# Keeping plain float32 blocks of the first token half in a two-layer trunk kernel

## The chip, the cores and the metric

The kernel runs on one core of one Trainium2 chip. The metric is the device time of one execution in microseconds (us). The engines of the core work side by side and wait for each other through semaphores: TensorE (PE in the profile, with its weight loads as PEld) multiplies matrices, VectorE (DVE) and ScalarE (ACT) work element by element, GpSimd (POOL) does the same more slowly, and SyncE (SP) issues most of the DMAs. TensorE writes its products into PSUM banks; all else lies in SBUF tiles.

## The reference

The program is a trunk of two layers on 1024 tokens of width 1024. Layer 0 mixes tokens with a gated delta net, layer 1 with retention; behind each mixer stands a convolutional feed-forward block. Cut to what matters here:

```python
e = jax.nn.silu(c @ cond_w + cond_b)
for i in range(DEPTH):
    mod = (e @ ada_w[i] + ada_b[i])[:, None, :]
    sh1, sc1, g1, sh2, sc2, g2 = jnp.split(mod, 6, axis=-1)
    y = mixers[i % N_MIXERS](x * (1.0 + sc1) + sh1)
    x = layer_norm(DN_ALPHA * x + (1.0 + g1) * y, ln_g[i, 0], ln_b[i, 0])
    y = conv_ffn(x * (1.0 + sc2) + sh2, ffn_up[i], ffn_conv_w[i], ffn_conv_b[i], ffn_down[i])
    x = layer_norm(DN_ALPHA * x + (1.0 + g2) * y, ln_g[i, 1], ln_b[i, 1])
```

The change lies where `x * (1 + sc) + sh` is made ready for the large products behind it: for `ffn_up` of both layers and for the retention's `w_in`.

## The kernel before

**Products in three parts.** Every large float32 product is made of products of a faster type (`float32r`): each operand is split into a high half, a copy in that type by ScalarE (line 89), and a low half, the rest, by a subtraction on VectorE (line 90). Three products, low by high, high by low and high by high, then give one (`mm3`, lines 108 to 112).

**The stages.** Three times an input of 8 feature blocks by 1024 tokens meets a weight: stage A (feed-forward of layer 0), B (retention) and C (feed-forward of layer 1). The blocks are feature-major, 128 features by 512 tokens. With f the feature block (0 to 7) and k from 0 to 3, block 11 is f = k of the first token half, 21 is f = 4 + k of the first half, 12 and 22 are the same of the second half.

**The build.** The blocks of the first half (11 and 21) are made by `build_one` (line 279) while the projection before is still running on the second half: four transposes on TensorE into an mm bank (line 282), a scale and shift by ScalarE into a tile `tmp` of tag "t2" (line 284), and the split. In A that projection is `proj_ln`, in B and C it is `proj_gen`, which calls the build as hooks in its sixth product.

**The seven-product scheme.** `strassen` (line 1290) first computes two pairs of weight units in the plain way, by `side`: over the first half, and, when the second half's blocks are there, over the second half (line 1309). All other items run through `wino` (line 1357 and on), which needs seven products instead of eight and, for that, the sums T1 = 12 - 11, T3 = 22 - 12, T2 = T3 + 11 and T4 = 21 - T2. `build_T` makes the blocks 12 and 22 (transposes at line 439, scale and shift at line 441, splits); its inner function `rest`, called between the two side products of the second half, makes the T blocks. There the plain values of 12 and 22 are still at hand (`raw`), but those of 11 and 21 exist only as two halves. `whole` puts such a block together again: two products of a unit matrix with the high and with the low half, added in an mm bank (line 457), 8 blocks or 16 products per stage.

For each k, `rest` then runs on VectorE and ScalarE: a sum (line 464), the split of T3, a sum with block 11 from the bank (466), the split of T2, a sum (468), the split of T1, a sum with block 21 from the bank (470), the split of T4. Each split is a copy on ScalarE followed by the subtraction on VectorE.

**Buffers.** Tiles are taken from rings by tag: "t2" has 3 buffers, "qkv" 20, of 128x512 float32 each, mm has 2 PSUM banks. "qkv" holds the T3 and T4 blocks (16 buffers in the end), four of the raw blocks, and in the projection of B and C the loads and the halves of the last steps. In A and C, the T1, T2 and 12 blocks share the 8 buffers of "hTb".

**Order.** Instructions stand on each engine in an order that the framework's scheduler makes from the order of the program, the dependences, the free buffers and its own estimate of durations; each engine works its list in order. Only parts of the mixers and of the retention's output projection (`run`, `pq`) have an order written out by hand. `anchor` marks an instruction behind which others on the same engine are to stand.

Of the kernel before, what the change touches and what calls it, by code (L numbers as in the profile page):

```python
# [10 lines left out]
F32R = mybir.dt.float32r  # L11
AF = mybir.ActivationFunctionType
ALU = mybir.AluOpType
AX = mybir.AxisListType

P = 128
D = 1024
S = 1024
KT = D // P
HALF = 512  # L20
# [8 lines left out]
BAL = {"r11": 0, "r12": 0, "r22": 0, "rS1": 0, "rS2": 0, "rS3": 0, "rS4": 0, "rw21": 0, "rwT1": 0, "rwT2": 0, "rwT3": 0, "rwT4": 0, "rn": 0, "rh": 1, "011": 0, "012": 0, "022": 0, "0S1": 0, "0S2": 0, "0S3": 0, "0S4": 0, "0w21": 0, "0wT1": 0, "0wT2": 0, "0wT3": 0, "0wT4": 0, "0n": 1, "0h": 0, "f11": 0, "f12": 0, "f22": 0, "fS1": 0, "fS2": 0, "fS3": 0, "fS4": 0, "fw21": 0, "fwT1": 0, "fwT2": 0, "fwT3": 0, "fwT4": 0, "fn": 1, "fh": 0, "gw": 99, "gh": 0, "gn": 3, "b1": 0, "b2": 0, "b3": 0, "b4": 0, "bT": 0, "ba": 0, "rw11": 0, "rw22": 0, "0w11": 0, "0w22": 0, "fw11": 0, "fw22": 0}  # L29
# [4 lines left out]
def trunk_kernel(ctx: ExitStack, tc, A):  # L34
    nc = tc.nc
    pe, act, dve, pool, sp = nc.tensor, nc.scalar, nc.vector, nc.gpsimd, nc.sync
# [9 lines left out]
    def tl(tag, shape, dt=F32, name=None):  # L46
        return sb.tile(shape, dt, tag=tag, name=name or tag, bufs=BUFS[tag])

    def two(tag, dt=F32, name=None):
        if tag in ("qkv", "auh"):  # L50
            return tl(tag, [P, HALF], dt, name), tl(tag, [P, HALF], dt, name)
        t = tl(tag, [P, 2, HALF], dt, name)
        return t[:, 0], t[:, 1]
# [7 lines left out]
    def mm_tile():  # L61
        return ps.tile([P, HALF], F32, tag="mm", name="mm", bufs=2)
# [25 lines left out]
    def split(dst_h, dst_l, src, eng=dve):  # L88
        anchor["sp"] = act.activation(dst_h, src, AF.Copy)  # L89
        eng.tensor_tensor(dst_l, src, dst_h, ALU.subtract)  # L90

    anchor = {}
# [74 lines left out]
    def col_sum(a, n, tile):  # L167
        pt = tile()
        for j in range(n):
            pe.matmul(pt[:, j:j + 1], a[:, j * P:(j + 1) * P], ones[:, 0:1], start=True, stop=True)  # L170
        return pt
# [22 lines left out]
    ident, m_incl, m_low = [cst[:, i * P:(i + 1) * P] for i in range(3)]  # L194
# [5 lines left out]
    pt = col_sum(a0, NV, mm_tile)  # L200
# [75 lines left out]
        dve.tensor_add(shift, shift, sh)  # L276
        return scale, shift

    def build_one(tag, xts, scale, shift, f, eng=dve):
        pt = mm_tile()  # L280
        for t in range(4):
            pe.transpose(pt[:, t * P:(t + 1) * P], xts[t][:, f * P:(f + 1) * P], ident)
        tmp = tl("t2", [P, HALF])
        act.activation(tmp, pt, AF.Identity, bias=shift[:, f:f + 1], scale=scale[:, f:f + 1])
        ht = two(tag, F32R, "hT")
        split(ht[0], ht[1], tmp, eng)
        return ht

    def build_hT(tag, xts, scale, shift, fr=range(KT)):
        return [build_one(tag, xts, scale, shift, f) for f in fr]  # L290
# [93 lines left out]
    def ln_store(half, t, xts, dst, key):  # L384
        r0 = half * HALF + t * P
        anchor[key] = act.dma_start(dst[r0:r0 + P, :], xts[t])
# [31 lines left out]

    def ln_hooks(half, xts, tag, vecs2, out, dst, key, npool=0):
        def build(f):  # L420
            out.append(build_one(tag, xts, *vecs2(), f, pool if f < npool else dve))
        return ([lambda f=f: build(f) for f in range(KT)]
                + [lambda t=t: ln_store(half, t, xts, dst, key) for t in range(4)])

    def build_T(B, xts, scale, shift, tags):
        tags = dict(zip(("T1", "T2", "T3", "T4", "22"), tags))
        tags["12"] = tags["T1"]
        for nm in tags:
            B[nm] = [None] * 4

        def put(nm, k, src, eng=dve):
            t = two(tags[nm], F32R, nm)
            split(t[0], t[1], src, eng)
            B[nm][k] = t

        def load(f, tag):
            pt = mm_tile()
            for t in range(4):
                pe.transpose(pt[:, t * P:(t + 1) * P], xts[t][:, f * P:(f + 1) * P], ident)
            tmp = tl(tag, [P, HALF], name="bt")  # L440
            act.activation(tmp, pt, AF.Identity, bias=shift[:, f:f + 1], scale=scale[:, f:f + 1])
            return tmp

        raw = []
        for k, tg in enumerate((("qkv", "qkv"), ("qkv", "qkv"), ("t2", "t2"), ("t2", "ada"))):
            b12, b22 = load(k, tg[0]), load(4 + k, tg[1])
            put("12", k, b12, pool if BAL["b3"] & 1 << k else dve)
            put("22", k, b22, pool if BAL["b2"] & 1 << k else dve)
            raw.append((b12, b22))

        one = tl("S", [P, P], F32R, name="one")
        act.activation(one, ident, AF.Copy)

        def whole(b, k):
            pt = mm_tile()
            for i, x in enumerate(B[b][k]):
                pe.matmul(pt, one, x, start=(i == 0), stop=(i == 1))
            return pt

        def rest():  # L460
            for k in range(4):
                t1, b22 = raw[k]
                x11 = whole("11", k)
                dve.tensor_sub(b22, b22, t1)
                put("T3", k, b22, pool if BAL["b3"] & 1 << k else dve)
                dve.tensor_add(b22, b22, x11)
                put("T2", k, b22, pool if BAL["bT"] & 1 << k else dve)
                dve.tensor_sub(t1, t1, x11)
                put("T1", k, t1, pool if BAL["b1"] & 1 << k else dve)
                dve.tensor_sub(b22, whole("21", k), b22)  # L470
                put("T4", k, b22)

        return rest

# [815 lines left out]
    def strassen(hT0, xts, scale, shift, items, tags=("hTb", "hTb", "qkv", "qkv", "aux"), direct=False, late=()):  # L1290
# [23 lines left out]
        for n in (1, 0):  # L1314
# [11 lines left out]
            for t, x in zip(ahead[n], X):  # L1326
                act.activation(t, x, AF.Copy)
        rest = build_T(B, xts, scale, shift, tags)

        def block(src):  # L1330
# [463 lines left out]
    for nh in range(2):  # L1794
        pt = mm_tile()
# [16 lines left out]
    h0, xts = layer_tail(0, raws, A["gdn_wout"], xin, xs[0], xs[1], next0, False)  # L1812
# [46 lines left out]
    def gate_item(u):  # L1859
        def start():  # L1860
            def sink(q, a, b):
                c = c_of(q, a, b) if b is not None else tl("cv", [P, 516], name="sg")[:, 0:HALF]
                act.activation(c, a if b is None else c, AF.Silu)
                act.dma_start(gd[u + q // 2][:, hs(q % 2)], c)
            return sink
        return A["ret_wg"][u], A["ret_wg"][u + 1], start, None
# [5 lines left out]
    B = strassen(h0, xts, sc_r, sh_r, [gate_item(0), gate_item(2)] + mixed, ("hTa", "aux", "qkv", "qkv", "hTa"), True)  # L1872
    hT = [h0, []]
    xlo = []
    for t in range(4):
        x = tl("cv", [P, 516], name="xlo")[:, 0:HALF]
# [302 lines left out]
```

## Time and profile before

| | |
|---|---|
| time, median of 3 runs | 2877.69 us (2877.47 to 2882.09) |
| profiled execution, first to last instruction | 2868.4 us, 38930 instructions |
| granted TensorE clock, mean | 0.995 |
| unit-matrix products in stage A | 737.4 to 762.7 us |
| in stage B | 1406.0 to 1431.6 us |
| in stage C | 2232.3 to 2259.4 us |

The page gives the profiled execution by its span, from the first to the last instruction; its own time is not listed apart. Times in rows are us from the start of the span unless a row gives mean nanoseconds. `mm<-hT,one` reads: writes tile mm, reads tiles hT and one. A group's row ends with the engine's idle time in front of the group and what ended most of it. In an order of time, the square bracket holds the idle time just before that instruction and its releaser.

### The profile page before, as it was taken

The page shows a single profiled execution, that of the slowest core. Times are in us where ns is not written, and L with a number is a line of the kernel's source. Part 1 is how long each engine was busy: PE and PEld are TensorE (multiplying, and loading weights), DVE is VectorE, ACT ScalarE, POOL GpSimd, SP SyncE. Part 2 cuts the span into 40 slices and gives each one's busy share as a digit, 9 for nine tenths or more (in the row PEclk, how much of TensorE's full clock was granted, in tenths as well). Part 3 has the DMA queues.
Part 4 walks back from the last instruction along what each step waited for, and adds up shares of the span by engine and source line. Part 5 has one row for each costly group of instructions (what it writes and reads, how often), then busy time and mean ns, then how long its engine had stood idle before and what let it go on. Part 6 is the DMA issues. An engine that isn't in the chain of part 4 may idle for free.

```text
span 2868.4 us, 38930 instructions
## 1 busy us (share of the span) xinstructions
PE 2780.8 (97%) x13594; PEld 2273.7 (79%) x13594; DVE 2177.9 (76%) x3874; ACT 1298.0 (45%) x2387; POOL 499.8 (17%) x513
## 2 busy tenths in 40 slices
PE   8999999999999999999999999999999999999997
PEld 6788878887787878887788887777777788888886
DVE  6787778676788888868687656666689887777779
ACT  4664465344645444545433342222344644445543
POOL 0311321000023322000000002333201033332201
PEclk9999999999999999999999999999999999999999
DMA  7223242174255554855343364665754253444753
GB/s 279 89 96 122 92 139 90 64 255 148 96 186 176 189 181 164 299 161 182 129 147 125 118 202 153 200 209 159 256 200 150 74 195 132 144 140 165 285 184 116
DMA packets 252884, 465.30 MB, mean 162 GB/s; under 512 B 24144, under 2 KB 77776, under 8 KB 252688
## 3 DMA queue, kind: packets, MB, share of 16 engines
q1 hardware_dynamic: 218560, 408.02, 43.0%
q10 hardware_dynamic: 31488, 46.15, 4.4%
q0 software_dynamic: 2640, 8.65, 0.8%
q8 instruction: 107, 1.75, 0.2%
q14 instruction: 89, 0.73, 0.1%
HBM read 346.86 MB, written 115.87 MB: 161 GB/s over the span
## 4 chain that ended last, share of the span: by engine, by line
PE 61%; DVE 20%; DMA 9%; ACT 5%; issue 4%; POOL 1%; SPq 0%; ACTq 0%; DVEq 0%; POOLq 0%
PE acc L716 11%; PE acc L1296 6%; PE acc L110 5%; PE acc L111 4%; PE acc L112 4%; PE sc L716 4%; PE sc L1296 3%; PE acc L1596 3%; PE mm L716 2%; DVE o L1742 2%; DVE wb L90 2%; PE sc L110 2%; PE sc L112 2%; PE sc L111 2%; DMA mvw<-in_ada_w 1%
## 5 line engine op out<-in xcount | busy, mean ns | idle before, releaser
L716 PE MATMUL acc<-hT,wh 128*128 128x512 f32 x960 | 299.4, 393 | 0.0
L1596 PE MATMUL acc<-bb,ab 128*128 128x512 f32 x984 | 229.7, 392 | 7.0 <-DVE ab L90 4.7
L89 ACT ACTIVATE ab<-ar 128x512 fp32r<-128x512 f32 x210 | 131.2, 630 | 221.3 <-PE mm L303 52.1
L1596 PEld LDWEIGHTS acc<-bb,ab 128*128 128x128 f32 x984 | 183.0, 188 | 49.0 <-DVE ab L90 4.2
L716 PEld LDWEIGHTS acc<-hT,wh 128*128 128x128 f32 x960 | 182.0, 190 | 35.5
L90 DVE TENSOR_TENSOR ab<-ar,ab 128x512 fp32r<-128x512 f32 x210 | 147.4, 707 | 76.5 <-ACT ab L89 76.3
L1296 PE MATMUL acc<-T,wb 128*128 128x512 f32 x840 | 202.0, 389 | 0.4 <-DVE wb L90 0.4
L89 ACT ACTIVATE wb<-mm 128x512 fp32r<-128x512 f32 x216 | 124.4, 597 | 166.0 <-DVE mm L1350 154.5
L716 PE MATMUL acc<-hT,wl 128*128 128x512 f32 x480 | 196.2, 409 | 2.2 <-ACT sq L509 2.2
L1296 PEld LDWEIGHTS acc<-T,wb 128*128 128x128 f32 x840 | 157.5, 188 | 33.8 <-ACT o L1743 1.2
L90 DVE TENSOR_TENSOR wl<-wr,wh 128x1024 fp32r<-128x1024 f32 x98 | 122.2, 1247 | 74.6 <-ACT wh L89 74.0
L1773 POOL TENSOR_TENSOR o<-o 128x512 f32<-128x512 f32 x80 | 126.2, 1586 | 266.4 <-ACT pc L1366 173.1
L90 DVE TENSOR_TENSOR wb<-wr,wb 128x512 fp32r<-128x512 f32 x162 | 115.3, 713 | 67.6 <-ACT wb L89 67.5
L89 ACT ACTIVATE wh<-wr 128x1024 fp32r<-128x1024 f32 x98 | 103.8, 1060 | 137.1 <-PE acc L716 56.4
L1742 DVE SCALAR_TENSOR_TENSOR o<-g,vc,o 128x512 f32<-128x512 f32 (+2 forms) x176 | 148.8, 855 | 8.4 <-ACT o L1737 7.1
L90 DVE TENSOR_TENSOR wb<-mm,wb 128x512 fp32r<-128x512 f32 x216 | 144.6, 682 | 7.8 <-ACT wb L89 7.8
L89 ACT ACTIVATE wb<-wr 128x512 fp32r<-128x512 f32 x162 | 101.1, 626 | 95.4 <-PE acc L1296 27.5
L1350 DVE TENSOR_TENSOR mm<-wr 128x512 f32<-128x512 f32 x108 | 83.6, 774 | 70.3 <-DMA wr<-in_ffn_up 57.7
L716 PE MATMUL acc<-wh,hT 128*128 128x512 f32 x384 | 134.3, 412 | 2.1 <-DVE vv L90 2.1
L1366 ACT ACTIVATE pc<-acc 128x512 f32<-128x512 f32 x143 | 84.5, 591 | 108.5 <-PE acc L1296 64.1
L239 DVE SCALAR_TENSOR_TENSOR ada<-mvw,e,ada 128x512 f32<-128x512 f32 x140 | 105.4, 753 | 24.9 <-DMA mvw<-in_ada_w 24.6
L110 PE MATMUL acc<-T,wb 128*128 128x512 f32 x292 | 114.4, 392 | 3.7 <-DVE wb L90 3.6
(675 smaller groups left out, 7343.0 us busy)
## 6 DMA issues: line engine op xcount, KB each, us to landing
wr<-in_ffn_up SPq DMA_DIRECT2D x92, 512.0 KB, 3.9
mvw<-in_ada_w SPq DMA_DIRECT2D x80, 512.0 KB, 4.3
ad<-o SPq DMA_DIRECT2D x154, 256.0 KB, 2.3
ar<-ad SPq DMA_DIRECT2D x154, 256.0 KB, 3.7
Br<-in_ffn_down SPq DMA_DIRECT2D x88, 256.0 KB, 3.6
wr<-in_ret_wv SPq DMA_DIRECT2D x32, 512.0 KB, 3.6
ar<-od SPq DMA_DIRECT2D x56, 256.0 KB, 5.2
wr<-in_gdn_wqkv SPq DMA_DIRECT2D x24, 512.0 KB, 3.6
```

The costliest lines, as they stand in the source:

```text
L89: anchor["sp"] = act.activation(dst_h, src, AF.Copy)
L90: eng.tensor_tensor(dst_l, src, dst_h, ALU.subtract)
L110: mm(acc, wl[:, k], hl[0], start=first, stop=False)
L111: mm(acc, wh[:, k], hl[1], start=False, stop=False)
L112: mm(acc, wh[:, k], hl[0], start=False, stop=last)
L239: dve.scalar_tensor_tensor(a, wr[:, kk], e[:, k:k + 1], a, ALU.mult, ALU.add)
L716: pq(pe.matmul(out, lhsT, rhs, start=start, stop=stop), cost or COST[out.shape[-1]])
L1296: return pe.matmul(*a, skip_group_check=True, **kw)
L1366: act.activation(t, X, AF.Copy)
L1596: return pe.matmul(*args, skip_group_check=True, **kw)
L1742: dve.scalar_tensor_tensor(tv, gv[:, c0 - j:c1 - j], w[:, 2 - j:3 - j], tv, ALU.mult, ALU.add)
L1773: (dve if fp == 0 else pool).tensor_tensor(o[d], o[x], o[y], op)
```

## The change

`build_one` gets a parameter for the tag of its plain block. For the first token half the tag is "qkv" instead of "t2", and the block is kept in a list instead of being dropped after its split. `build_T` takes the eight kept blocks over as `low`; the unit matrix in float32r, `whole` and its products go. In `rest`, block 11 is read from `low[k]` and block 21 from `low[4 + k]`; T4 is written over the latter. The four high halves are copied as soon as each sum stands, T1 comes before T2, and the low halves are subtracted later, that of T4 in the next round of k.

```diff
-    def build_one(tag, xts, scale, shift, f, eng=dve):
+    kept = []
+
+    def build_one(tag, xts, scale, shift, f, eng=dve, home="t2"):
...
-        tmp = tl("t2", [P, HALF])
+        tmp = tl(home, [P, HALF])
         act.activation(tmp, pt, AF.Identity, bias=shift[:, f:f + 1], scale=scale[:, f:f + 1])
         ht = two(tag, F32R, "hT")
         split(ht[0], ht[1], tmp, eng)
+        if home != "t2":
+            kept.append(tmp)
         return ht
...
-            out.append(build_one(tag, xts, *vecs2(), f, pool if f < npool else dve))
+            out.append(build_one(tag, xts, *vecs2(), f, pool if f < npool else dve, "t2" if half else "qkv"))
...
-        one = tl("S", [P, P], F32R, name="one")
-        act.activation(one, ident, AF.Copy)
-
-        def whole(b, k):
-            pt = mm_tile()
-            for i, x in enumerate(B[b][k]):
-                pe.matmul(pt, one, x, start=(i == 0), stop=(i == 1))
-            return pt
+        low = kept[:]
+        del kept[:]
 
         def rest():
+            part = {}
+
+            def hi(nm, k, src):
+                t = part[nm, k] = two(tags[nm], F32R, nm)
+                anchor["sp"] = act.activation(t[0], src, AF.Copy)
+                B[nm][k] = t
+
+            def lo(nm, k, src):
+                t = part.pop((nm, k))
+                dve.tensor_tensor(t[1], src, t[0], ALU.subtract)
+
+            last = None
             for k in range(4):
                 t1, b22 = raw[k]
-                x11 = whole("11", k)
                 dve.tensor_sub(b22, b22, t1)
-                put("T3", k, b22, pool if BAL["b3"] & 1 << k else dve)
-                dve.tensor_add(b22, b22, x11)
-                put("T2", k, b22, pool if BAL["bT"] & 1 << k else dve)
-                dve.tensor_sub(t1, t1, x11)
-                put("T1", k, t1, pool if BAL["b1"] & 1 << k else dve)
-                dve.tensor_sub(b22, whole("21", k), b22)
-                put("T4", k, b22)
+                hi("T3", k, b22)
+                dve.tensor_sub(t1, t1, low[k])
+                hi("T1", k, t1)
+                if last:
+                    lo("T4", k - 1, last)
+                lo("T3", k, b22)
+                dve.tensor_add(b22, b22, low[k])
+                hi("T2", k, b22)
+                lo("T1", k, t1)
+                lo("T2", k, b22)
+                last = low[4 + k]
+                dve.tensor_sub(last, last, b22)
+                hi("T4", k, last)
+            lo("T4", 3, last)
```

## The prediction

> **What bounds the kernel now.** I read the page first, its busy shares and its chain, then the costliest groups with shapes kept apart, then the three places where the removed products stand.
>
> ```profile
> PE 2780.8 (97%) x13594; PEld 2273.7 (79%) x13594; DVE 2177.9 (76%) x3874; ACT 1298.0 (45%) x2387; POOL 499.8 (17%) x513
> PE 61%; DVE 20%; DMA 9%; ACT 5%; issue 4%; POOL 1%; SPq 0%; ACTq 0%; DVEq 0%; POOLq 0%
> L457 PE MATMUL mm<-hT,one 128*128 128x512 f32 x48 | 15.3, 410 | 1.4 <-ACT bt L441 1.0 <-DVE bt L470 0.3
> ```
>
> TensorE is busy 97% of the span and holds 61% of the chain; VectorE is next with 20%. The change takes out the third row: 48 products, 16 in each of three stages, which I call A (feed-forward of layer 0), B (retention) and C (feed-forward of layer 1). A busy TensorE need not be a full one, so I looked at how many products start in ten microseconds.
>
> ```profile
> 740.00:750.00 10.00, 9.17 (x41) 7.27 (x40) 8.30 (x13) 5.96 (x11) 0.00 (x0) 1.00 0.05 10
> 750.00:760.00 10.00, 10.00 (x46) 8.20 (x45) 8.53 (x13) 4.49 (x8) 0.00 (x0) 1.00 0.28 97
> 780.00:790.00 10.00, 10.00 (x46) 8.27 (x45) 10.00 (x17) 4.90 (x8) 0.00 (x0) 1.00 0.38 146
> 1410.00:1420.00 10.00, 8.76 (x38) 6.60 (x37) 7.80 (x11) 4.65 (x7) 0.00 (x0) 1.00 0.33 113
> 1420.00:1430.00 10.00, 10.00 (x46) 8.21 (x45) 8.86 (x16) 6.54 (x12) 0.00 (x0) 1.00 0.26 86
> 1450.00:1460.00 10.00, 10.00 (x46) 8.14 (x44) 10.00 (x18) 2.52 (x6) 0.00 (x0) 1.00 0.62 178
> 2240.00:2250.00 10.00, 8.68 (x37) 6.56 (x36) 8.45 (x12) 5.17 (x8) 0.00 (x0) 1.00 0.25 75
> 2250.00:2260.00 10.00, 10.00 (x45) 8.24 (x45) 7.56 (x13) 4.82 (x8) 0.00 (x0) 1.00 0.08 32
> 2280.00:2290.00 10.00, 10.00 (x45) 8.01 (x44) 10.00 (x18) 7.07 (x13) 0.00 (x0) 1.00 0.34 119
> ```
>
> These are windows inside the three stages; after the width stand busy time and starts of TensorE, its weight loads, VectorE and ScalarE. Two things are to be seen. Where TensorE waits for nothing it starts 45 or 46 products, one each 0.22 us, so there it is full; the 410 ns of the group is a product's length in the pipe, not its price. And in the window with most L457 rows of each stage it starts only 37 to 41: something waits there. VectorE, with 10.00 of 10, is full some 20 to 40 us behind the removed products.
>
> The Trainium skill, page "Perfetto Trace Analysis", section "Identifying the Most-Contended Engine", says that matmul occupancy does not tell how near TensorE is to its limit and that the weight-load share does. By its measure the 79% above would leave a fifth of TensorE open, and removed products could be worth nothing; the 46 starts in ten microseconds speak against that in the full windows, and the 37 to 41 for it in the others.
>
> **The change part by part.** *Removed products.* What one costs is read from the chain of waits, and which of them are hidden from the order of time.
>
> ```profile
> 754.14 0.47 PE mm L457 x2
> 738.53 0.73 PE L457 MATMUL mm<-hT,one 128*128 128x512 f32 x2 [0.52 <-ACT bt L441]
> 746.47 1.09 PE L457 MATMUL mm<-hT,one 128*128 128x512 f32 x4
> 748.39 0.50 PE L110 MATMUL acc<-12_6961,wl 128*128 128x512 f32 x1 [0.83 <-DVE wl L90]
> 1414.71 1.34 PE L457 MATMUL mm<-hT,one 128*128 128x512 f32 x4
> 1417.30 0.50 PE L110 MATMUL acc<-12_12747,wl 128*128 128x512 f32 x1 [1.24 <-DVE wl L90]
> 2234.51 1.20 PE L457 MATMUL mm<-hT,one 128*128 128x512 f32 x4 [0.52 <-ACT bt L441]
> 2242.46 1.09 PE L457 MATMUL mm<-hT,one 128*128 128x512 f32 x4
> 2243.87 0.73 PE L457 MATMUL mm<-hT,one 128*128 128x512 f32 x2 [0.32 <-DVE bt L470]
> 2245.61 0.50 PE L110 MATMUL acc<-12_19796,wl 128*128 128x512 f32 x1 [1.00 <-DVE wl L90]
> ```
>
> The first row is of the chain: a pair costs 0.47 us. The others are TensorE in order of time; in square brackets stands what it waited for. In each stage some L457 rows stand right in front of a wait for the low half of the next weight unit (0.83, 1.24 and 1.00 us): 4 in A, 4 in B, 6 in C. Without them TensorE reaches that wait sooner and waits longer, so they are worth nothing. The other 12 + 12 + 10 = 34, or 17 pairs, stand in a full stream: 17 x 0.47 = 8.0 us. In A and C one pair besides waits 0.52 us for a bank behind the L441 copy; with no product to place there those two waits go too: 1.0 us. The weight load behind the long wait is set off by the end of the products before it, so it moves up with them. What is late next is that same load, already counted, and behind it the last T1 blocks.
>
> *Sums and halves on VectorE.* The counts stay: four sums, four copies of high halves and four low halves per k. Only the second operand of three of the sums moves from a bank to a kept block.
>
> ```profile
> L464 DVE TENSOR_TENSOR bt<-bt x12: 678/688/694, 727.9 to 2238.3; 128x512 f32<-128x512 f32 x12
> L466 DVE TENSOR_TENSOR bt<-bt,mm x12: 681/688/690, 738.0 to 2256.8; 128x512 f32<-128x512 f32 x12
> L90 DVE TENSOR_TENSOR T<-bt,T 128x512 fp32r<-128x512 f32 x48 | 31.5, 686 | 14.3 <-ACT T L89 14.1
> L89 ACT ACTIVATE T<-bt 128x512 fp32r<-128x512 f32 x48 | 28.9, 631 | 18.8 <-DVE bt L470 12.8 <-DVE bt L466 4.9 <-PE acc L112 0.5
> ```
>
> A sum with a bank operand (L466) and one without (L464) have the same median, 688 ns, so the move costs and gains nothing. The Trainium skill, page "VectorE: DVE Perf Modes", section "The TRN2 errata", gives 120 fixed cycles for a PSUM source against 58 for SBUF, an estimate of 65 ns for each of 36 sums, 2.3 us of VectorE; the two medians do not agree with it. The last two rows show the ping-pong that the new order aims at: VectorE idles 14.1 us in front of low halves for the high half just asked for, ScalarE 12.8 us for the last sum. In the new order each low half stands behind another sum. That is idle time of engines off the chain, so I price it at nothing by itself (at most the 14.1 us if VectorE set the pace throughout), but it pays for the next point.
>
> *Does VectorE follow?* TensorE comes some 2.7 us earlier to each full stretch of VectorE (8.0 + 1.0 over three). Before those stretches VectorE idles, by the windows above, 1.70 + 1.47 = 3.2 us in A, 2.20 + 1.14 = 3.3 in B, 1.55 + 2.44 = 4.0 in C. So there is room to follow, but hardly more than is needed. I take off 1.0 us for what does not fit (between 0, if all idle closes, and 6 us, if VectorE moves by a third only).
>
> *Kept blocks.* Eight per stage now live in the 20 "qkv" buffers from the build until the sums, not in the three of "t2".
>
> ```profile
> L284 ACT ACTIVATE t<-mm,fh,fs x8: 761/772/802, 1335.6 to 1357.3; 128x512 f32<-128x512 f32 x8
> 1335.62 1.43 ACT L284 ACTIVATE t<-mm,fh,fs 128x512 f32<-128x512 f32 x2
> ...
> 1340.90 0.76 ACT L284 ACTIVATE t<-mm,fh,fs 128x512 f32<-128x512 f32 x1
> ...
> 1354.13 0.78 ACT L284 ACTIVATE t<-mm,fh,fs 128x512 f32<-128x512 f32 x1 [1.11 <-DVE hT L90]
> 1350.00:1360.00 10.00, 7.95 (x36) 6.12 (x36) 10.00 (x18) 6.77 (x11) 0.59 (x1) 1.00 0.59 211
> L1429 SPq DMA_DIRECT2D ar<-ad x13: 319/319/655, 1299.7 to 1339.6; - x13
> DMA to landing us min/median/max: 2.4/3.6/9.2
> L1429 SPq DMA_DIRECT2D ar<-od x16: 319/320/320, 2101.4 to 2170.4; - x16
> L284 ACT ACTIVATE t<-mm,fh,fs x8: 762/770/782, 2189.7 to 2205.9; 128x512 f32<-128x512 f32 x8
> ```
>
> These are the build (L284) and the loads of the projection running beside it (L1429), in B and then in C. In C the last load is out at 2170.4, the first kept block comes at 2189.7: no clash. In B six of the eight builds come after the last load at 1339.6. There the same buffers hold eight halves of the projection's tail, so a late build may wait for a buffer; the one wait of today, 1.11 us for "t2", goes in exchange. TensorE starts only 36 products in that window. Zero is my value, the bounds are 1.1 us either way, with the rival below beyond. SP's loads behind such a buffer wait in order, those of the next weights among them. In A the build beside the output projection finds the eight buffers of the first half free.
>
> *Copy of the unit matrix.* Three ScalarE copies on an engine that is 45% busy: nothing. The two mm banks that held the products come free for the first weight sums of the next stretch: between nothing and one more wait of the 0.52 us kind per stage, taken as nothing.
>
> Sum: 8.0 + 1.0 - 1.0 = 8.0 us. The span of 2868.4 us becomes 2860.4. The median of the runs, 2877.69, lies 9.3 us above that span, which is outside the first and last instruction and stays: 2869.7 us.
>
> **The rivals.** *VectorE does not follow* (R1). The stretches with 10.00 of 10 keep their place, since the idle before them comes from other waits: the blocks named 12, whose buffers the last T blocks take over only when the side products have read them, and weight loads.
>
> ```profile
> 1440.86 5.08 DMA wr<-in_ret_wqk
> 768.43 1.98 DVE o L1742 x3
> ```
>
> For it: the chain leaves TensorE just there, for a load in B and for VectorE's convolution in A. This is also where the weight-load measure would be right. Then about a third of 9 us is left, 3 us: 2874.7.
> *More than the sum* (R2). Removing the rows in front of the waits lets the scheduler finish one side product earlier, so the waits for the low half close too: 24 pairs x 0.47 = 11.3, the two 0.52 and 0.83 + 1.24 + 1.00 = 3.1, together 15.4 us: 2862.3 at most. Against it: nothing in the trace shows that order changing.
> *Kept blocks starve the projection in B* (R3, slower). If the builds come before the last loads, 8 kept and 8 tail buffers leave 4 of 20 for loads. A step is then a load of 3.6 us, a copy of 0.63 and a low half of 0.69, 4.9 us, against 12 products at 0.23, 2.7 us. Over 7 steps that is 15.4 us lost: 2885.1. It decides from the point where the eighth build is in front of the fifth-last load; today two are. That the change leaves products in place is no rival: L457 is gone from the code.
>
> **How the numbers follow.** Forecast 0.48 (2866 to 2872), R1 0.28, R2 0.13, R3 0.11. A measurement of this kernel can tell about 0.2%, 5.8 us, from no change. Forecast and R2 are faster by more, 0.61; R1 is the same, 0.28; R3 slower, 0.11. The range runs from near R2's bound past R1, to no change and the 1.1 us of a buffer wait: 2863.5 to 2878.5; it leaves out R3 and the edge of R2.
>
> **What would show it.** No L457 row; TensorE's count 13594 down by 48; in the three windows the starts up from 37 to 41 towards 46, or the wait for the low half longer by the hidden rows (R1 in small). VectorE's 14.1 us in front of T halves mostly gone. The distance from L439's last row to the first full window of each stage shorter by some 2.7 us, and kept so to the next stage; if it is shorter and then given back by waits for weight halves, R1 is right. In B, L284 and L1429 rows waiting for each other show R3. A schedule that differs far from the three places would make the prediction wrong in either direction.

## The result, and the profile after

| | time, median | range | runs |
|---|---|---|---|
| before | 2879.89 us | 2877.47 to 2884.66 | 4 |
| after | 2907.44 us | 2906.33 to 2911.24 | 4 |

The ratio is 1.0105, with a 95% interval of 1.009 to 1.0119: the change makes the kernel slower, by 25.9 to 34.3 us of 2879.9. The prediction was faster, 2869.7 us, and its range ended at 2878.5.

From the two pages, the rows of the projection's products before, then the busy times and the same rows after (lines have moved: 1596 is now 1612, 1429 is 1445, 1462 is 1478, 282 is 284, 284 is 286):

```profile
L1596 PE MATMUL acc<-bb,ab 128*128 128x512 f32 x984 | 229.7, 392 | 7.0 <-DVE ab L90 4.7
L1596 PEld LDWEIGHTS acc<-bb,ab 128*128 128x128 f32 x984 | 183.0, 188 | 49.0 <-DVE ab L90 4.2
```

```profile
PE 2790.3 (96%) x13546; PEld 2278.9 (78%) x13546; DVE 2182.5 (75%) x3874; ACT 1296.8 (45%) x2384; POOL 496.5 (17%) x513
L1612 PE MATMUL acc<-bb,ab 128*128 128x512 f32 x984 | 234.9, 398 | 12.0 <-DVE ab L90 12.0
L1612 PEld LDWEIGHTS acc<-bb,ab 128*128 128x128 f32 x984 | 187.3, 192 | 57.6 <-DVE ab L90 18.5
```

TensorE has its 48 instructions fewer, and yet 9.5 us more busy time. The projection's products (L1612) wait longer for their operands: 12.0 and 57.6 us, against 7.0 and 49.0 before. The averages say no more than that; a loss of 1% has to be looked for by place.

I laid the n-th TensorE instruction of one profiled execution beside the n-th of the other, the removed products left out. By the clock of the kernel before, the one after is 5.5 us late at 785 us (A's sums are through) and 6.0 at 1300 us; then 15.2 at 1372 us, when the projection ahead of B is over; 13.9 at 2156 us, in the projection ahead of C, 33.3 at its end (2212 us), and 37.8 once C's sums are through (2277 us). Counted in the same way at 500 us, where the change has not yet come in, the profiled executions of all kernels of this document lie 0 to 6.5 us behind that of before, so only the two steps at the projections of B (9) and C (19) say something by themselves. Neither is in the sums, where the change takes its products out.

The projection ahead of C, first the kernel before, then the kernel after: SyncE's waits from 2100 to 2215 us, as total, times and longest in us.

```profile
SPq L1462 <- DVE ab L90: 29.3, 12, 4.0
SPq L1429 <- DVE ab L90: 21.1, 11, 3.2
```

```profile
SPq L1445 <- DVE ab L90: 30.0, 13, 10.5
SPq L1445 <- DMA xs<-xt: 25.4, 2, 24.3
```

Before, a load of the projection waits only for a buffer, at most 4.0 us. After, one load waits 24.3 us, and what ends its wait is the store of the normalized rows (`ln_store`). SyncE in order of time, kernel after:

```profile
2151.31 0.32 SPq L1445 DMA_DIRECT2D ar<-od  x1
2154.03 0.33 SPq L1478 DMA_DIRECT2D Br<-in_ret_wout  x1
2178.75 0.32 SPq L1445 DMA_DIRECT2D ar<-od  x1
2180.07 0.33 SPq L1478 DMA_DIRECT2D Br<-in_ret_wout  x1
```

For 24.7 us no operand is loaded. What TensorE and ScalarE do meanwhile, in order of time, with the idle time before an instruction in brackets (TensorE first):

```profile
2176.04 0.69 PE L284 MATMUL mm<-cst,xt 128*128 128x128 f32 x2 [4.39 <-DVE xt L314]
...
2185.97 0.66 PE L284 MATMUL mm<-cst,xt 128*128 128x128 f32 x4 [0.53 <-ACT qkv L286]
2186.38 3.00 PE L1612 MATMUL acc<-bb,ab 128*128 128x512 f32 x12
```

```profile
2166.25 0.63 ACT L89 ACTIVATE bb<-Br 128x512 fp32r<-128x512 f32 x1 [1.56 <-PE acc L1612]
2176.02 3.00 ACTq L390 DMA_DIRECT2D xs<-xt  x4
2179.20 1.45 ACT L286 ACTIVATE qkv<-mm,fh,fs 128x512 f32<-128x512 f32 x2 [12.32 <-PE mm L284]
```

All 32 transposes of the build now stand in one piece in TensorE's list, ahead of the rest of the projection. They need normalized rows (xt), which come at 2176; TensorE is empty for 4.39 us, does the transposes at a slow pace, and goes on at 2186. ScalarE has the stores and the first block in front of its next operand splits and waits 12.32 us. Before, the same 32 transposes lie spread among the products, in order of time:

```profile
2179.42 0.44 PE L282 MATMUL mm<-cst,xt 128*128 128x128 f32 x2
2180.74 0.44 PE L282 MATMUL mm<-cst,xt 128*128 128x128 f32 x2 [0.88 <-DVE xt L310]
2181.43 3.01 PE L1596 MATMUL acc<-bb,ab 128*128 128x512 f32 x12 [0.25 <-DVE ab L90]
2184.28 0.38 PE L282 MATMUL mm<-cst,xt 128*128 128x128 f32 x2
2184.41 3.68 PE L1596 MATMUL acc<-bb,ab 128*128 128x512 f32 x15
```

From here the projection after lives from load to load. The groups of the operand load in that window, of the kernel before (its line stands in the prediction, last start 2170.4) and after:

```profile
L1445 SPq DMA_DIRECT2D ar<-od x30: 319/320/782, 2099.9 to 2212.9; - x30
DMA to landing us min/median/max: 2.5/5.4/7.0
```

The last load is issued 42.5 us later than before, of which 13.9 were there already. So the question is what moved the builds: where the blocks are asked for, how many buffers they hold, the new order of the sums, or the missing products.

### The profile page after: what moved, and what is told of

Its sections match the earlier page's. It is cut to its first block, busy times and chain, and to the rows that moved or that the text cites. A ratio compares the mean times of both kernels' runs of the same rounds, so it can differ in the third digit from the quotient of the medians.

```text
span 2909.5 us, 38785 instructions
## 1 busy us (share of the span) xinstructions
PE 2790.3 (96%) x13546; PEld 2278.9 (78%) x13546; DVE 2182.5 (75%) x3874; ACT 1296.8 (45%) x2384; POOL 496.5 (17%) x513
## 4 chain that ended last, share of the span: by engine, by line
PE 60%; DVE 22%; DMA 8%; ACT 5%; issue 4%; POOL 0%; SPq 0%; ACTq 0%; DVEq 0%; POOLq 0%
PE acc L732 11%; PE acc L1312 6%; PE acc L110 4%; PE acc L111 4%; PE acc L112 4%; PE sc L732 4%; PE acc L1612 4%; PE sc L1312 3%; DMA wr<-in_ffn_up 3%; PE mm L732 2%; DVE o L1758 2%; DVE wb L90 2%; DVE mm L1366 2%; PE sc L110 1%; PE sc L111 1%
## 5 line engine op out<-in xcount | busy, mean ns | idle before, releaser
L1612 PE MATMUL acc<-bb,ab 128*128 128x512 f32 x984 | 234.9, 398 | 12.0 <-DVE ab L90 12.0
L1612 PEld LDWEIGHTS acc<-bb,ab 128*128 128x128 f32 x984 | 187.3, 192 | 57.6 <-DVE ab L90 18.5
L1312 PEld LDWEIGHTS acc<-T,wb 128*128 128x128 f32 x840 | 157.6, 188 | 33.3 <-ACT pc L1382 0.6
L239 DVE SCALAR_TENSOR_TENSOR ada<-mvw,e,ada 128x512 f32<-128x512 f32 x140 | 105.7, 755 | 24.7 <-DMA mvw<-in_ada_w 24.4
```

Of the source, the lines that this page charges most:

```text
L239: dve.scalar_tensor_tensor(a, wr[:, kk], e[:, k:k + 1], a, ALU.mult, ALU.add)
L1312: return pe.matmul(*a, skip_group_check=True, **kw)
L1612: return pe.matmul(*args, skip_group_check=True, **kw)
```

## The experiments

Each was timed beside the kernel before; a ratio below 1 is faster. "Pair" means the two unit-matrix products that rebuild one block; there are 8 in a stage, 24 in all. Some expectations were written with "product" for pair.

| run | blocks kept in | pairs left | ratio to before, 95% interval |
|---|---|---|---|
| after | qkv: 8 in A, B, C | 0 | 1.0105 [1.009, 1.0119] |
| e1_order | none, new order of the sums | 24 | 0.9993 [0.998, 1.0006] |
| e4_keepA | qkv: 8 in A | 16 | 1.0004 [0.9993, 1.0015] |
| e4_keepB | qkv: 8 in B | 16 | 1.0013 [1.0003, 1.0023] |
| e4_keepC | qkv: 8 in C | 16 | 1.0059 [1.0041, 1.0077] |
| e2_homeC | none; 8 of C pass through qkv | 24 | 1.0031 [1.002, 1.0043] |
| e7_holdC | none; 8 empty buffers held in C | 24 | 1.0044 [1.0031, 1.0056] |
| e6_auhC | C: 6 in auh, 2 in qkv | 16 | 1.0077 [1.0063, 1.0091] |
| e3_double | none, old order, pairs twice | 48 | 1.0001 [0.9988, 1.0014] |
| e12_oneC | C: 1 in qkv | 23 | 1.0037 [1.0025, 1.0049] |
| e13_sixC | C: 6 in auh | 18 | 1.0006 [0.9997, 1.0014] |
| e14_other | auh: 4 in A, 6 in B, 6 in C | 8 | 1.0008 [0.9999, 1.0017] |
| e15_one21 | as e12_oneC, 21 buffers in qkv | 23 | 1.0045 [1.0032, 1.0059] |
| e16_order21 | as e1_order, 21 buffers in qkv | 24 | 0.9986 [0.9975, 0.9998] |

One thousandth is 2.88 us.

### Which part of the change, and which stage

The theory at the start: the kept blocks take buffers of qkv from the loads. The first run keeps the products and takes only the new order of the sums (its edit is shown against the kernel after, cut; the lines that build `one` and `whole` are back too); the next three take the new order, and keep blocks in one stage each.

```diff
 # e1_order, in rest(): the new order, block 11 and 21 still rebuilt
-                dve.tensor_sub(t1, t1, low[k])
+                dve.tensor_sub(t1, t1, x11)
...
-                last = low[4 + k]
-                dve.tensor_sub(last, last, b22)
+                last = b22
+                dve.tensor_sub(b22, whole("21", k), b22)
 # e4_keepC, in ln_hooks (A: stage 1, B: stage 2)
+        home = "t2" if half or len(stage) not in (3,) else "qkv"
```

> The kernel before with only the new order of the sums, high halves and low halves of rest(); the 48 unit-matrix products stay and no block is kept. Theory (the eight kept blocks take buffers of qkv from the loads of the projection): nothing of the loss is here, 2876 to 2884 us beside 2880. Rival (the new order of the sums is what costs): about 2900 to 2910, the whole of the loss or most of it.

> New order everywhere, blocks kept in stage A alone (its builds stand beside a projection that loads nothing into qkv), products in B and C. Theory: no starved loads, so between the forecast's gain of a third (2877) and the 5 us that the trace shows lost in A: 2876 to 2886. Rival (a stage loses whatever loads stand beside it, about a third of 27.5 us): 2889.

> New order everywhere, blocks kept in stage B alone. Theory: the projection of B pays for the eight buffers, +7 to +10 us by the two traces: 2886 to 2891. Rival (the loss sits in the order, or in each stage alike): equal to e1_order, or +9 in every one of A, B and C.

> New order everywhere, blocks kept in stage C alone. Theory: this is the dear one, +19 in the projection by the two traces and +4 in the sums: 2899 to 2905. Rival (the loss sits in the order, or in each stage alike): equal to e1_order, or 2889.

The order of the sums costs nothing: 0.9993, between 5.8 us faster and 1.7 us slower. Keeping costs by stage, against before: A 1.2 us (-2.0 to 4.3), B 3.7 (0.9 to 6.6), C 17.0 (11.8 to 22.2). The three steps beyond the run of the order add up: 11 + 20 + 66 ten-thousandths, less the 7 of the order itself, give 1.0090, near the 1.0105 of the whole change. Of these steps two thirds are C's. B came in below what was expected (2884.03 us where 2886 to 2891 was written), C just below (2898.79 against 2899 to 2905), and A gained none of its third of the forecast.

### Asking or holding

Two halves of keeping, each by itself, in C alone and with all products in place (the edits are against e4_keepC and cut; the second also reads each held buffer on GpSimd in `rest`, so that it stays taken): blocks that pass through qkv and are given back after the split, and eight buffers that are held and nearly empty while the builds stay in t2.

```diff
 # e2_homeC, in build_one: written to qkv, not kept
-        if home != "t2":
-            kept.append(tmp)
 # e7_holdC, in ln_hooks: build to t2, hold a buffer of qkv beside it
+            if home != "t2":
+                pinned.append(tl("qkv", [P, HALF], name="hold"))
+                pool.memset(pinned[-1][:, 0:4], 0.0)
```

> As the run that keeps blocks in C alone, but nothing is kept: in C the eight blocks of the first half are written to qkv and given back right after their split, and the 16 products of C stay. Theory (what hurts is that eight buffers are asked for ahead of later loads and stand empty until the normalized rows come): most of the loss of C stays, 2890 to 2899 us. Rival (what hurts is that the blocks are held to the end of the sums): the loss goes, 2876 to 2881.

> The other half of it: in C each build writes to t2 as in the kernel before, and beside it one buffer of qkv is taken, of which GpSimd fills four columns, and is held until the sums read them; the 16 products of C stay. Theory (empty buffers): as dear or less, the holding alone also takes eight of 20 buffers from the loads, 2882 to 2899 us. Rival (only the order in which the scheduler sets the builds): 2876 to 2881. If the number of buffers is all that counts, it is at least as dear as the run that keeps the blocks, 2899 or more.

Both cost: 8.9 us (5.8 to 12.4) and 12.7 us (8.9 to 16.1). The first was a little under the 2890 to 2899 written for it (2888.55 us) and far above the rival. Here nothing is kept and no product is gone, so a block need not be held to do harm. The second is not clean: in its trace GpSimd's fills themselves wait 80.3 us in eight waits for the operand buffers, ScalarE's build then waits 7.5 us for the low half that GpSimd makes behind them, and no load of the projection waits for a store. So it does not show what eight missing buffers cost by themselves: how much of the 12.7 us is theirs and how much GpSimd's list stays open. That holding adds to asking is suggested by the pair e2_homeC, 1.0031, and e4_keepC, 1.0059, whose intervals just touch and which differ in the eight pairs as well.

### Another ring, and the price of the products

If missing buffers of qkv were the cause, six blocks in the ring auh should have saved most of C.

```diff
 # e6_auhC, in ln_hooks
-            out.append(build_one(tag, xts, *vecs2(), f, pool if f < npool else dve, home))
+            out.append(build_one(tag, xts, *vecs2(), f, pool if f < npool else dve, home if home == "t2" or f > 5 else "auh"))
 # e3_double, in whole() of the kernel before
+            for r in range(2):
+                for i, x in enumerate(B[b][k]):
+                    pe.matmul(pt, one, x, start=(i == 0), stop=(i == 1))
```

> As the run that keeps blocks in C alone, but six of the eight go to the ring auh, of which the gate rows of the projection hold two buffers, and two to qkv. Theory: a quarter of the buffers and so a quarter of the loss of C or less, and the 16 products are gone: 2872 to 2882 us. Rival (keeping is dear because the products' removal leaves TensorE empty, wherever the blocks lie): 2895 or more.

> The kernel before with each of the 48 unit-matrix products issued twice (the second pair writes the same sums over the first). It prices the products: if they stand in TensorE's way as the forecast said for 17 of 24 pairs, +8 to +11 us, 2888 us; if all that stand are hidden or the work before and behind them hides them, 2878 to 2882 us, and then their removal was never worth the 8 us of the forecast.

Six in auh and two in qkv cost 22.2 us (18.1 to 26.2), no less than eight in qkv: my expectation of 2872 to 2882 us fell. In the projection ahead of C it is now not the operand loads but the rows' own loads (L301, `load_row`) that wait for a store; the operand loads stand behind them in SyncE's list, and none is issued from 2151.6 to 2186.4 us. SyncE's longest wait there:

```profile
SPq L301 <- DMA xs<-xt: 29.0, 3, 26.7
```

And doubling the products costs nothing that can be measured, 1.0001, at most 4.0 us. TensorE's waits in C's sums show where the added pairs went (kernel before, then e3_double, 2225 to 2265 us):

```profile
PE mm L439 <- ACT bt L441: 1.2, 2, 0.7
PE acc L110 <- DVE wl L90: 1.0, 1, 1.0
PE mm L457 <- ACT bt L441: 0.5, 1, 0.5
```

```profile
PE mm L439 <- ACT bt L441: 1.0, 2, 0.5
PE acc L110 <- ACT 12_19868 L89: 0.2, 1, 0.2
```

Eight pairs more, and the waits for the weight's low half and of the products themselves are gone: they have been filled. Over 2225 to 2300 us TensorE's waits fall from 4.2 us in sum to 1.4, which takes up 2.8 of the 3.8 us that eight pairs are by the row of 0.47. With the price of the products at nothing, and the number of buffers taken from the loads no explanation, a second theory: the requests of one ring are served in the order in which the program makes them. The build of the sixth product asks for a buffer of qkv before the loads of later steps do. Those cannot be set ahead of it, and it waits for normalized rows; so it is not the count that matters but that there is any request of qkv there at all. In e6_auhC there were two.

### One block

> As the run that keeps blocks in C alone, but one block instead of eight: only the first build of C goes to qkv and is kept, the other seven go to t2, and 15 of the 16... that is, seven of the eight products of C stay. Theory, as it now stands (requests of one ring are served in their order, so every load of qkv asked for later stands behind the first build, and the builds come in one piece ahead of the projection's last products): one block costs most of what eight cost, 2888 to 2899 us. Rival (what counts is how many of the 20 buffers are missing): an eighth of the 20 us, 2878 to 2884.

> As the run with six blocks in auh and two in qkv, but the two go to t2 and are rebuilt by products: C asks for nothing more in qkv. Theory (order of requests in qkv): the loss of 23 us is gone whole, 2872 to 2881 us. Rival (keeping six blocks, or the missing products, costs it): 2890 to 2903.

> The change without qkv: four blocks of A, six of B and six of C are kept in auh, the other eight are rebuilt by products; 16 of the 24 products are gone, and no order of the projections is moved. Theory, with the doubled products having cost nothing: the same as the kernel before, 2874 to 2882 us. Rival (the products that are gone give the forecast's price of 0.47 us each where they stood in the way, some 5 to 8 us): 2870 to 2874.

```diff
 # the last argument of build_one in ln_hooks: e12_oneC, e13_sixC, e14_other
+ home if home == "t2" else "qkv" if f < 1 else "t2"
+ home if home == "t2" else "auh" if f < 6 else "t2"
+ home if home == "t2" else "auh" if f < (4 if len(stage) == 1 else 6) else "t2"
```

One block in qkv costs 10.7 us (7.2 to 14.1), two thirds of what eight cost there. Six blocks in auh, with the two left over going to t2, cost 1.7 us (-0.9 to 4.0) where six and two in qkv had cost 22.2. The two kernels differ in nothing but the home of two blocks, and in the two pairs that rebuild them. The traces agree: SyncE's waits of e12_oneC and of e13_sixC, 2100 to 2215 us.

```profile
SPq L1459 <- DMA xs<-xt: 39.4, 2, 37.9
```

```profile
SPq L1492 <- DVE ab L90: 31.2, 13, 4.0
SPq L1459 <- DVE ab L90: 21.1, 11, 3.2
```

With one block in qkv a load stands still for 37.9 us; with six blocks elsewhere no load waits for a store, and the rows are nearly those of the kernel before (29.3 and 21.1 us there). The groups of the build's transposes, durations as min/median/max in ns and first and last start (e12_oneC, then e13_sixC):

```profile
L285 PE MATMUL mm<-cst,xt x32: 421/422/478, 2170.3 to 2181.0; 128*128 128x128 f32 x32
```

```profile
L285 PE MATMUL mm<-cst,xt x32: 270/272/323, 2188.9 to 2213.9; 128*128 128x128 f32 x32
```

In one piece of 11 us, and early, in the first; spread over 25 us in the second, as in the kernel before.

The run e14_other is the change without its side effect: 16 of 24 pairs gone, no request of qkv. At 1.0008 it is the same as before (at best 0.3 us faster; its median, 2882.89 us, lies 0.9 above what was written). The rival, 5 to 8 us from the missing products, is out.

### One buffer more

What one kept block still left open: it also leaves the loads 19 buffers of 20. With 21 they have their 20 again.

```diff
-    BUFS = {"hTa": 8, "hTb": 8, "qkv": 20, "aux": 4, "auh": 8, "lane": 4, "cv": 4, "ada": 1,
+    BUFS = {"hTa": 8, "hTb": 8, "qkv": 21, "aux": 4, "auh": 8, "lane": 4, "cv": 4, "ada": 1,
```

> As the run with one block of C kept in qkv, with 21 buffers in qkv instead of 20, so that the loads have the same 20 as in the kernel before. Theory (the place of the request in its ring moves the builds): the loss stays, 8 to 13 us over the run of the same ring with no kept block. Rival (one buffer too few for the loads tips the schedule): the loss is gone, within 4 us of that run.

> The baseline for it: only the new order of the sums, all products, no kept block, and 21 buffers in qkv. Theory and rival alike: 2872 to 2881 us; what it differs from the run with 20 buffers is what one buffer more is worth to the whole kernel.

The loss stays: 1.0045 with the block against 0.9986 without it, some 17 us between the two, above the 8 to 13 written. SyncE's waits of e15_one21 and e16_order21 in the same window:

```profile
SPq L1459 <- DMA xs<-xt: 41.7, 2, 40.6
```

```profile
SPq L1448 <- DVE ab L90: 26.6, 12, 4.4
SPq L1481 <- DVE ab L90: 21.7, 11, 3.2
```

So the count of buffers is out as the reason for what one block costs, and the request itself is left: with it the builds come first, without it, in either size of the ring, they do not. That the ring is served in the order of the requests is what these runs lead to; no run sets the request itself behind the loads. e16_order21 is also the fastest of all kernels run here, 4.0 us below before (0.6 to 7.2), less than the 0.2% that the prediction set as its bound; it keeps no block.

## Why the prediction was wrong, point by point

**Kept blocks, "no clash" in C (the step that failed).** The prediction compared the last load (2170.4) with the first kept block (2189.7) and found that the one is over before the other begins. That is a reading of a schedule in which the block is no request of qkv. Once it is one, the schedule is another: loads end at 2212.9, the transposes and the stores of the rows come first. The term was 0 with 1.1 us either way; with the new order alone as the base it measured about 19 us in C, 5.8 in B and 3.2 in A, the last within its error.

**R3, kept blocks starve the projection in B.** Right in kind and sign, wrong in place and in what decides. B was priced at 15.4 us and measured 3.7; C was held free and measured 17.0. R3 reckoned with buffers, "8 kept and 8 tail buffers leave 4 of 20". One block with all 20 left for the loads does the harm as well. B shows the same wait, SyncE from 1290 to 1400 us, kernel after:

```profile
SPq L1445 <- DMA xs<-xt: 28.7, 2, 27.4
```

Why 27.4 us without loads cost B only a fifth of what they cost C was not tried. One difference is seen: in B the normalized rows come from ScalarE, and TensorE waits for them 0.8 us at the longest, against 4.39 in C (its waits from 1300 to 1400 us, kernel after):

```profile
PE mm L284 <- ACT xt L312: 2.7, 4, 0.8
```

**Removed products, 17 x 0.47 = 8.0 us.** Wrong by nearly all of it. If 17 of 24 pairs stood in the way, 24 pairs more would have cost some 8.0 us, and they cost 4.0 at most. If their removal had paid, e14_other would have gained some 16 / 24 x 8.0 = 5.3 us, and it gained 0.3 at most. The same bound takes in the 1.0 us of the two waits of 0.52, and it leaves nothing of R2. The prediction counted as hidden only the pairs right in front of a wait. But TensorE's stream of the sums, however full in some windows, ends in waits for halves that VectorE and ScalarE make, and time gained ahead of them is handed over there. The waits of e13_sixC in C's sums (2225 to 2275 us) show it, beside the 1.0 us of the kernel before:

```profile
PE acc L110 <- DVE wl L90: 2.4, 1, 2.4
PE acc L110 <- DVE wb L90: 1.4, 1, 1.4
```

The prediction had a sign for just this, the wait for the low half of the weight longer by the hidden rows, and it came in all three stages. It was 0.83, 1.24 and 1.00 us in A, B and C; with pairs gone in e14_other it is 2.0, 2.4 and 2.4, and with all gone in the kernel after 2.4, 2.5 and 2.4; the new order alone (e1_order) has 0.8, 1.2 and 1.4 (the rows of e14_other in A, then of the kernel after in B):

```profile
PE acc L110 <- DVE wl L90: 2.0, 1, 2.0
```

```profile
PE acc L110 <- DVE wl L90: 2.5, 1, 2.5
```

**VectorE follows, less 1.0 us.** It does not follow: the wait above is for a half that VectorE makes. R1 had this mechanism and still left 3 us too many. One step of the sum is also off by itself: (8.0 + 1.0) over three stages is 3.0 us, not the 2.7 written, and 3.0 nearly uses up the 3.2 us of room in A. The rule of the Trainium skill that the prediction weighed, page "Perfetto Trace Analysis", section "Identifying the Most-Contended Engine" (occupancy of matmuls does not tell how near TensorE is to its limit; operations against the peak and the share of weight loads do), fits what was measured: removed products were worth nothing in a kernel whose weight loads filled 79%. The 46 starts in ten microseconds, held against it, are the state of some windows, not of the stage.

**Sums from a bank or from a kept block cost the same.** Right. The sum of T2 with a kept block (L480, after, 735 to 2300 us) and with a bank (L483, e1_order):

```profile
L480 DVE TENSOR_TENSOR bt<-bt,qkv 128x512 f32<-128x512 f32 x12 | 8.3, 689 | 0.2
```

```profile
L483 DVE TENSOR_TENSOR bt<-bt,mm 128x512 f32<-128x512 f32 x12 | 8.2, 684 | 0.2
```

**New order priced at nothing.** Right within 0.2%, but not for the reason given. VectorE's wait for the high half was to go "mostly"; with the new order alone it stayed, and only in the kernel after, with blocks at hand, did it fall from 14.1 to 8.5 us (e1_order, then after, where the 12 halves of T4 have a group of their own with no wait):

```profile
L470 DVE TENSOR_TENSOR T<-bt,T 128x512 fp32r<-128x512 f32 x48 | 31.7, 688 | 16.2 <-ACT T L465 16.0
```

```profile
L468 DVE TENSOR_TENSOR T<-bt,T 128x512 fp32r<-128x512 f32 x36 | 23.9, 683 | 8.5 <-ACT T L463 8.5
```

**Signs to look for.** L457 gone and TensorE's count down by 48: right. Starts towards 46 in the three windows: no; the other half of that sign, the longer wait, came. "L284 and L1429 rows waiting for each other show R3": this was the right sign, and it came in C as well.

**9.3 us outside the span.** Wrong. The profiled execution of the kernel after took 2911.24 us with a span of 2909.5, so 1.7 us lie outside. By that the profiled execution of before took some 2870 us and was faster than the timed runs; in later comparisons single runs of that kernel reach from 2872.53 to 2887.19 us.

What stays open: how C's 17 us divide among TensorE's empty 4.39 us, the late loads and the slower clock (below), how much of the step from one block to eight is the holding, and whether the loss goes if the build's request is moved behind the loads.

## What to carry to other kernels

Before a tile moves to another ring, ask who asks for that ring later in the program and could until now be set ahead of it: one request that must wait for late data can hold up all loads behind it, however many buffers are free. A trace shows when things happened under the old requests; it does not show that they may still happen so. And the price of an operation on a busy engine can be tried by doubling it before anything is rewritten: here twice as much cost nothing, and taking two thirds of it away brought nothing.

## What the runs showed that was not expected

**The clock falls where TensorE waits.** The 128x128 transposes take 272 ns each in the kernel before and 421 in the kernel after (groups of C's build, before, then after):

```profile
L282 PE MATMUL mm<-cst,xt x32: 270/272/335, 2179.4 to 2205.6; 128*128 128x128 f32 x32
```

```profile
L284 PE MATMUL mm<-cst,xt x32: 272/421/477, 2176.0 to 2186.4; 128*128 128x128 f32 x32
```

Windows of the kernel after, in C and then in B, with starts in brackets and the granted clock third from the end:

```profile
2170.00:2180.00 10.00, 4.40 (x16) 2.18 (x14) 7.93 (x19) 0.80 (x2) 3.20 (x4) 0.70 0.32 128
2180.00:2190.00 10.00, 8.36 (x38) 6.46 (x39) 7.37 (x11) 10.00 (x18) 1.27 (x1) 0.79 0.97 317
2190.00:2200.00 10.00, 10.00 (x46) 8.26 (x45) 7.30 (x13) 5.38 (x11) 0.00 (x0) 1.00 0.98 370
2220.00:2230.00 10.00, 7.56 (x21) 5.96 (x22) 9.77 (x14) 2.12 (x2) 0.00 (x0) 0.57 0.44 142
```

```profile
1320.00:1330.00 10.00, 6.23 (x26) 4.09 (x25) 3.19 (x14) 9.06 (x12) 1.62 (x3) 0.70 0.76 285
1330.00:1340.00 10.00, 8.56 (x31) 6.79 (x30) 8.55 (x14) 8.49 (x15) 0.59 (x1) 0.62 0.79 265
```

The clock is 1.00 throughout these stretches of the kernel before. So a wait costs more than its length. The mean granted clock is 0.985 to 0.986 in the four runs of the kernel after, and 0.993 in the middle of the 29 runs of the kernel before beside e1_order; 0.007 of 2907 us is some 20 us at full clock, an estimate and an upper bound of what the slower clock costs directly, since TensorE is partly empty in these stretches.

A long gap is not needed for it. In C the first fall stands at the empty 4.39 us, but the last row, 0.57, comes behind waits of 0.77, 1.44 and 2.50 us, and in B no wait of TensorE from 1300 to 1400 us is over 1.4 us. The Trainium skill, page "TensorE: Matmul & The Clock Gate", part 1, gives half rate after an idle window of about 3.4 us. The trace does not bear out that a whole window must be empty: its clock record goes to half at 2173.9, 2.3 us into the gap, and ahead of these three falls TensorE was empty for 2.2 to 2.3 of 3.4 us.

**Loads that come late come together.** In the same rows the DMA share is 0.97 and 0.98 at 317 and 370 GB/s while the loads held back are issued, and a load's median time to landing is 5.4 us in that window, against 2.8 in e13_sixC. They are not only late but slow.

**A load waits for a store that it has nothing to do with.** The operand loads wait 24.3, 27.4, 37.9 and 40.6 us for "xs<-xt" in the rows above, yet they read or write neither. What couples them stands in the trace's single records, behind the views: the DMAs that SyncE and ScalarE issue share eight semaphores for their landing, numbered 100 to 104, 106, 108 and 109, which are used in turn, and a DMA that gets a number again waits until the one that had it has landed. In C of the kernel after, the four stores have 103, 104, 106 and 108, right behind the 102 of the load of 2126.8 us. Four more loads pass with 109, 100, 101 and 102; the fifth gets 103 and waits until the store of 2176.02 us has landed, at 2178.7, and the next three take the numbers of the other stores. B shows the same with 106, and so do e12_oneC and e15_one21 with 103. In the kernel before, the stores take their numbers behind the 103 of the last load. So here a store that was set early in the schedule stopped SyncE's loads before one turn of the eight was over, with buffers free or not.
